# The even mixer's 31-tap convolution: chunks moved from GpSimd to TensorE, with diagonal tap tiles loaded from DRAM

## The chip, the cores and the metric

One program on one core of a Trainium2 chip. The metric is the device time of one execution in microseconds, the median of several runs. The engines are called PE (TensorE; PEld is its weight loads), DVE (VectorE), ACT (ScalarE), POOL (GpSimd) and SP (SyncE, which here only issues DMAs).

## The reference, cut to what matters

The network has a first block of two transformer layers with experts, and a second block of two layers, each of a mixer, a cross-attention to a memory and an MLP. The mixer of the second block's first layer is the "even" mixer; 256 tokens of 1024 channels, all in fp32:

```python
def causal_depthwise_conv(x, w, b):          # here: w is [31, 1024], one filter of 31 taps for each channel
    width = w.shape[0]
    y = lax.conv_general_dilated(x, w[:, None, :], window_strides=(1,), padding=[(width - 1, 0)],
                                 dimension_numbers=('NWC', 'WIO', 'NWC'), feature_group_count=x.shape[-1])
    return y + b

def even_mixer(x, w_in, conv_w, conv_b, ...):
    proj = x @ w_in                                        # 1024 -> 4624 columns
    conv_val, conv_gate, z, xbc, dt = jnp.split(proj, ...)
    u = conv_val * jax.nn.sigmoid(conv_gate)
    u = causal_depthwise_conv(u, conv_w, conv_b)           # the convolution of this change
    u = jax.nn.silu(layer_norm_2(u, conv_ln_g, conv_ln_b)) # normalised over the 1024 channels
    xbc = jax.nn.silu(causal_depthwise_conv(xbc, ...))     # four taps
    ...                                                    # the state-space branch: y, gated by silu(z), normalised
    return jnp.concatenate([u, y], axis=-1) @ w_out
```

Each output of the convolution is a sum of 31 products, out[n, ch] = sum over j of w[j, ch] u[n - 30 + j, ch], plus a bias. The channels stand on the partitions in eight chunks of 128.

## The kernel before, in words

`even` (from L1119) is one pass over the mixer. Its dense products split each fp32 weight tile into a high part `wh` (ACT, L252) and a low part `wl` (DVE, L255), and do three matmuls for each pair of tiles (L363 to L365, or L289 to L291). Weights come as tiles of 128x2048 fp32 (1 MB) through `raw` (L224): three buffers in rotation, loads issued by SP in program order, each waiting until the buffer's last tile has been read.

In program order: `wvg` (eight tiles) gives value and gate; ACT takes a tanh, and DVE writes the gated value into `U` (L1148), two chunks at a time, with 30 zeros ahead of each chunk. Then `xbc` with its four taps (L1164 to L1175), a chain of 128x32 instructions for dt (L1183 to L1198), `z` (`wz`, four tiles), the state-space branch (L1238 to L1286), the convolution (L1288 to L1324), its normalisation (L1326 to L1355: sums of the channels by matmuls with ones, L1329 and L1343) and the product with `weo` (eight tiles; the state-space half of its rows, `caty`, first, then the half of the convolution, `catu`, in the rows the tiles `xt`).

A scheduler puts each engine's instructions into a fixed order ahead of time, so the convolution's instructions stand between those of the dense products. The eight chunks go three ways (L1787, L1290, L1312):

- chunks 4 and 7 on PE (L1291 to L1310). `cpair0` and `cpair1` hold 64 channels each: on partitions 0 to 63 the chunk as it is, on 64 to 127 the same shifted by one position, so that one matmul of 128 rows does two taps. Its weights are two 64x64 diagonals of taps, one under the other, which ACT makes into `cdiag`, one instruction for each (L1304). 16 tap pairs by two halves are 32 matmuls for a chunk, and the trace holds two records for each matmul; the halves write different partitions of one accumulator.
- chunks 0 and 3 on POOL, a multiplication into `cvt` and an addition for each tap (L1314 to L1324).
- chunks 1, 2, 5 and 6 on DVE, one multiply-add for each tap (L1322).

Of the kernel before, what the change touches and what calls it, by code (L numbers as in the profile page):

```python
# [26 lines left out]
OP = mybir.AluOpType  # L27
# [69 lines left out]
def layout(inp):  # L97
    g = {k: np.asarray(v) for k, v in inp.items()}
    o = {}
# [66 lines left out]
    o["convw2"] = np.ascontiguousarray(w.reshape(16, 2, 8, 2, 64).transpose(1, 4, 2, 3, 0)).reshape(128, 256)  # L166
# [19 lines left out]
class Net:  # L186
# [46 lines left out]
    @contextmanager  # L233
    def more_raw(self, n, side="left"):
        """n more tiles for weights in flight, while the block lasts"""
        with self.tc.tile_pool(name="rawx", bufs=1, side=side) as pool:
            i = self.slot % len(self.slots)
            self.slots = self.slots[i:] + self.slots[:i] + [(pool, f"rx{j}") for j in range(n)]
            self.slot = 0
            yield  # L240
            i = self.slot % len(self.slots)
            self.slots = [x for x in self.slots[i:] + self.slots[:i] if x[0] is not pool]
            self.slot = 0
# [18 lines left out]
    def split_x(self, dst, src, scale=None):  # L262
        """dst (hi, lo) views <- src fp32 view (SBUF or PSUM)"""
        hi, lo = dst
        nc = self.nc
        if scale is None:
            nc.scalar.activation(hi, src, AF.Copy)
            nc.vector.tensor_tensor(lo, src, hi.bitcast(F32), op=OP.subtract)
        else:
            nc.scalar.activation(hi, src, AF.Copy, scale=scale)  # L270
            nc.vector.scalar_tensor_tensor(lo, src, scale, hi.bitcast(F32), op0=OP.mult, op1=OP.subtract)

    def affine_split(self, dst, src, G, B, n):
        """blocks: dst[:, k] <- src[:, k] * G[:, k] + B[:, k]; src PSUM [128, n, w]"""
        hi, lo = dst
        nc = self.nc
        x = self.wk.tile([128, n, src.shape[-1]], F32, tag="afs", name="afs", bufs=2)
        for k in range(n):
            if B is None:
                nc.scalar.activation(x[:, k], src[:, k], AF.Copy, scale=G[:, k:k + 1])  # L280
            else:
                nc.scalar.activation(x[:, k], src[:, k], AF.Identity, scale=G[:, k:k + 1], bias=B[:, k:k + 1])
        nc.vector.tensor_copy(hi, x)  # L283
        self.last_split = nc.vector.tensor_tensor(lo, x, hi.bitcast(F32), op=OP.subtract)  # L284
# [8 lines left out]
    def dense_nat(self, units, tiles, evac, ncol=512, kper=4):  # L293
        """units: list of (xh, xl, token offset); tiles: [[DRAM tile per K group] per column chunk]"""
# [23 lines left out]
    def project(self, us, src, qs, finish):  # L318
        """finish(u, c, acc) for the halves c of 1024 columns, unit by unit; src[c, q]: weights of the K groups q"""
# [24 lines left out]
    def dense_tr(self, x, tiles, evac, tag="acc"):  # L344
        """x: (hi, lo) [128, 8, 256]; tiles: DRAM [128, 8*256]; evac(tile, psum [128, 2, 256])"""
        for c, src in enumerate(tiles):
            acc = self.bank(tag).rearrange("p (b n) -> p b n", b=2)
            self.tile_tr(x, self.raw(src), acc)
            evac(c, acc)
# [17 lines left out]
    def transpose_into(self, src, n, sink, tags=("tp",)):  # L367
        """src [128, n*128] -> banks of four [128, 128] blocks; sink(block offset, count, psum)"""
# [14 lines left out]
    def half_stats(self, key, z, c):  # L383
        """statistics of the half c of the rows z"""
        if c == 0:
            self.bst[key] = self.wk.tile([128, 2, 6], F32, tag="bst", name="bst", bufs=5)
        self.nc.vector.bn_stats(self.bst[key][:, c], z[:, c * 512:(c + 1) * 512])

    @contextmanager
    def later(self, n):  # L390
        """work of the block as if it came n instructions later"""
# [4 lines left out]
    def row_stats(self, key, eps):  # L396
        """(mean and variance, 1 / standard deviation) of rows whose halves half_stats has seen"""
# [4 lines left out]
    def norm_rows(self, key, z, eps):  # L402
        """z <- (z - mean) * rsqrt(var + eps) along the free axis"""
# [6 lines left out]
    def last_rows(self, key, z, eps, g, b, out):  # L410
        """out <- the normalised rows z times g plus b"""
# [43 lines left out]
    def mods(self, l, i):  # L455
        """a third of the modulation vectors of both streams, as columns: eight steps, to call one after the other;
        the four column groups of the PE array take 512 columns each"""
# [23 lines left out]
    def mods_rows(self, l, i, n):  # L481
        """the same third for the first n streams, by the sums of products along the free axis"""
# [26 lines left out]
    def bc_cols(self, cols):  # L509
        """[128, 512] PSUM <- the 512 entries of the columns [128, 4], on every partition"""  # L510
# [5 lines left out]
    def bc(self, l, i, s, out):  # L516
        """out [128, 1024] <- the modulation vector i of stream s on every partition"""
# [65 lines left out]
    def rope_to(self, x, t, nh):  # L583
        """x [128, nh, 64]; the two addends of its rotation"""
# [14 lines left out]
    def mixers(self, mg, gp, pool, l, streams, with_ctx, hook):  # L599
        """streams: {name: (xh, xl)}; mg[stream, token tile] <- twice the merged branches"""  # L600
# [29 lines left out]
        def place_q(m, s, t, q):  # L630
            """q [128, 2, 128]: the heads of g=0 and of g=1"""
# [34 lines left out]
        def chunk(src, ncol, kper, evac_full, ctx_cols):  # L666
            """one column chunk for the streams that need all of it; the ctx stream may need only ctx_cols"""
# [62 lines left out]
        # branch A  # L730
# [38 lines left out]
        # branch B and the queries of C  # L769
# [92 lines left out]
    def router(self, pool, l, fold, streams):  # L862
        """router weights times the modulated gain, and what the mean and the shift of the rows add"""
# [18 lines left out]
    def route(self, pool, l, zT, wg, add, stats, streams):  # L882
        """one-hot columns of each expert's tokens and the affinities; zT[s, half]: the rows before their
        normalisation, transposed; stats[s, t]: their means and standard deviations"""
# [67 lines left out]
    def experts(self, l, z, fold, streams, g2, gain, oh, af, rsc):  # L952
        """z[s] [128, 2, 1024], normalised, becomes ALPHA * h + g2 * (the experts' outputs at their tokens)"""
# [151 lines left out]
    def small_tr(self, pool, x, w, name):  # L1105
        """[16, 256 tokens] in SBUF <- x @ w for 16 columns, transposed"""
# [12 lines left out]
    def even(self, pool, x, finish):  # L1119
# [4 lines left out]
        cw2 = self.load(pool, "convw2t", I["convw2"], [128, 8, 2, 16])  # L1124
        ident2 = mk("ident2", [128, 64])
        nc.vector.tensor_tensor(ident2, self.ident[:, 0:64], self.ident[:, 64:128], op=OP.add)
# [22 lines left out]
        # state-space branch  # L1149
# [139 lines left out]
        for k in range(8):  # L1289
            if k in self.conv_pe:  # L1290
                acc = self.bank("acc")[:, :256]  # L1291
                ps = []
                for h in range(2):
                    hs = slice(64 * h, 64 * h + 64)
                    p = mk(f"cpair{h}", [128, 286])
# [4 lines left out]
                for m in range(0, 16, 2):  # L1300
                    d = mk("cdiag", [128, 2, 2, 64], 2)
                    for h in range(2):
                        for i in range(2):
                            nc.scalar.activation(d[:, h, i], ident2, AF.Copy, scale=cw2[:, k, h, m + i:m + i + 1])  # L1304
                    for i in range(2):
                        for h in range(2):
                            q = m + i
                            nc.tensor.matmul(acc[64 * h:64 * h + 64], lhsT=d[:, h, i], rhs=ps[h][:, 2 * q:2 * q + 256],
                                             start=q == 0, stop=q == 15, skip_group_check=True)
                nc.scalar.activation(cv[:, k], acc, AF.Identity, scale=0.5, bias=cb[:, k:k + 1])  # L1310
                continue
            pool_k = k in self.conv_pool  # L1312
            eng = nc.gpsimd if pool_k else nc.vector
            eng.tensor_scalar(cv[:, k], U[:, k, 0:256], cw[:, k, 0:1], None, op0=OP.mult)  # L1314
            for j in range(1, 31):
                if pool_k:
                    tm = mk("cvt", [128, 256], 2)
                    nc.gpsimd.tensor_tensor(tm, U[:, k, j:j + 256], cw[:, k, j:j + 1].to_broadcast([128, 256]),
                                            op=OP.mult)
                    nc.gpsimd.tensor_tensor(cv[:, k], cv[:, k], tm, op=OP.add)  # L1320
                else:
                    nc.vector.scalar_tensor_tensor(cv[:, k], U[:, k, j:j + 256], cw[:, k, j:j + 1], cv[:, k],  # L1322
                                                   op0=OP.mult, op1=OP.add)
            eng.tensor_scalar(cv[:, k], cv[:, k], 0.5, cb[:, k:k + 1], op0=OP.mult, op1=OP.add)  # L1324

        # normalisation of the convolution over channels  # L1326
# [355 lines left out]
    def residual(self, z, g, b, side="left"):  # L1682
        """z <- z * g + b, in place"""
# [15 lines left out]
    def mem_kv(self, i):  # L1699
        """a quarter of the memory's keys or values, to DRAM until they are needed"""  # L1700
# [76 lines left out]
    def build(self):  # L1777
        tc = self.tc
        with ExitStack() as self.ctx:
# [7 lines left out]
            self.conv_pe, self.conv_pool = (4, 7), (0, 3)  # L1787
# [29 lines left out]
```

## Time and profile before

| | |
|---|---|
| three timed runs | 2828.42, 2828.75, 2834.20 us; median 2828.75 us |
| the profiled execution | span 2830.3 us |
| busy over the span | PE 2479.0 us, DVE 1554.4 us, ACT 856.9 us, POOL 296.6 us |
| mean clock granted to PE | 0.918 of full speed |

The profiled execution's own time is its span; what lies around the first and last instruction is not shown, and 2830.3 lies among the three timed runs. In the page's 40 slices of 70.8 us the even mixer is slices 27 to 30, which for POOL read 7, 9, 0, 0 tenths busy. The stretch from the first gated value to the last product with `weo` runs from about 1866 to 2117 us of the span.

### The profile page before, as it was taken

The numbers are of one execution on the slowest core, as the hardware profiler recorded it, in microseconds if no ns is written. First come the engines' busy times: TensorE is split into PE (matmuls) and PEld (weight loads), VectorE is DVE, ScalarE is ACT, GpSimd is POOL, SyncE is SP. The second block draws the span as 40 slices with busy tenths as digits, with TensorE's granted clock in tenths as the row PEclk, the third lists the DMA queues.
The fourth block names the chain that finished last, engine by engine and source line by source line (L and its number), as shares of the span: only waits on it lengthen the run. The fifth ranks groups of instructions, "written<-read, shape, count | busy, mean of one in ns | idle before, by whom it ended". The sixth has DMA issues, their size and how long they took to land.

```text
span 2830.3 us, 35061 instructions
## 1 busy us (share of the span) xinstructions
PE 2479.0 (88%) x14042; PEld 1694.2 (60%) x14042; DVE 1554.4 (55%) x2586; ACT 856.9 (30%) x1485; POOL 296.6 (10%) x261
## 2 busy tenths in 40 slices
PE   7999999899899879998866777786999999998898
PEld 4667678552222227776412333376768898867797
DVE  4779886442222258756311222289976755656655
ACT  2343233210000014533100010132664544543443
POOL 0001120000000011010000000079001100201100
PEclk8999999999989889999877878787999999998999
DMA  7135555489999964546899999842255652543551
GB/s 285 63 132 181 168 214 216 175 332 412 421 421 421 422 275 148 189 140 245 371 427 426 425 426 426 373 145 86 75 181 195 224 190 87 187 181 130 198 182 42
DMA packets 115811, 695.75 MB, mean 246 GB/s; under 512 B 26288, under 2 KB 27184, under 8 KB 34752
## 3 DMA queue, kind: packets, MB, share of 16 engines
q1 hardware_dynamic: 113728, 687.22, 62.5%
q0 software_dynamic: 1920, 6.29, 0.6%
q8 instruction: 111, 1.82, 0.3%
q14 instruction: 52, 0.43, 0.0%
HBM read 688.22 MB, written 5.24 MB: 245 GB/s over the span
## 4 chain that ended last, share of the span: by engine, by line
PE 61%; DMA 18%; DVE 14%; issue 3%; ACT 3%; POOL 1%; SPq 0%; DVEq 0%; POOLq 0%; ACTq 0%
PE acc L291 9%; PE acc L289 9%; PE acc L290 9%; DMA raw<-in_wgu 8%; PE acc L1005 8%; PE acc L1037 5%; DMA raw<-in_wdn 4%; DVE wl L255 3%; PE att L364 2%; DMA raw<-in_xwk 2%; PE att L365 2%; PE att L363 2%; PE att L552 2%; PE tp L373 2%; PE att L579 2%
## 5 line engine op out<-in xcount | busy, mean ns | idle before, releaser
L255 DVE TENSOR_TENSOR wl<-raw,wh 128x1024 fp32r<-128x1024 f32 x384 | 485.9, 1271 | 281.7 <-ACT wh L252 274.6
L252 ACT ACTIVATE wh<-raw 128x1024 fp32r<-128x1024 f32 x384 | 403.8, 1058 | 578.1 <-PE acc L291 257.5
L1005 PE MATMUL acc<-raw,xs 128*64 128x512 f32 (+1 forms) x2048 | 379.9, 648 | 58.6 <-DMA raw<-in_wgu 58.3
L1005 PEld LDWEIGHTS acc<-raw,xs 128*64 128x64 f32 (+1 forms) x2048 | 99.4, 126 | 307.3 <-issue 180.0
L1009 ACT ACTIVATE eth<-acc 64x512 f32<-64x512 f32 x48 | 28.3, 590 | 671.7 <-PE acc L1005 671.7
L1011 DVE SCALAR_TENSOR_TENSOR esg<-eth,acc 64x512 f32<-64x512 f32 x48 | 32.7, 680 | 351.2 <-ACT eth L1009 350.7
L289 PE MATMUL acc<-wh,xtlath 128*128 128x512 f32 (+1 forms) x448 | 177.2, 396 | 9.8 <-DVE xtlath L283 6.7
L380 POOL TENSOR_TENSOR rs<-rs,mhalf 128x1 f32<-128x1 f32 (+3 forms) x36 | 31.7, 885 | 1446.1 <-DVE rs L379 1444.5
L291 PE MATMUL acc<-wh,xtlatl 128*128 128x512 f32 (+1 forms) x448 | 177.3, 397 | 1.8 <-DVE xtlatl L284 1.8
L290 PE MATMUL acc<-wl,xtlath 128*128 128x512 f32 (+1 forms) x448 | 177.0, 395 | 1.4 <-DVE wl L255 1.4
L492 DVE SCALAR_TENSOR_TENSOR junk<-raw,crow 128x1024 bf16<-128x1024 f32 x128 | 162.9, 1273 | 5.0 <-DMA raw<-in_wmt 4.2
L364 PE MATMUL acc<-xth,wl 128*128 128x256 f32 x416 | 128.7, 309 | 36.6 <-DVE wl L255 36.5
L363 PE MATMUL att<-xth,wh 128*128 128x256 f32 x512 | 145.7, 285 | 6.7 <-DVE xth L283 6.7
L1037 PE MATMUL acc<-raw,eaT 128*64 128x512 f32 x512 | 141.7, 717 | 10.3 <-DVE eaT L202 5.5
L364 PE MATMUL att<-xth,wl 128*128 128x256 f32 x512 | 145.5, 284 | 0.3 <-DVE wl L255 0.3
L365 PE MATMUL att<-xtl,wh 128*128 128x256 f32 x512 | 145.4, 284 | 0.0
L363 PE MATMUL acc<-xth,wh 128*128 128x256 f32 x416 | 127.3, 306 | 8.0 <-DVE xth L283 8.0
L365 PE MATMUL acc<-xtl,wh 128*128 128x256 f32 x416 | 126.6, 305 | 5.3 <-DVE xtl L284 5.3
L364 PEld LDWEIGHTS acc<-xth,wl 128*128 128x128 f32 x416 | 89.0, 214 | 40.4 <-DVE wl L255 39.6
L1048 DVE TENSOR_TENSOR eylat<-acc,g2lat 32x512 f32<-32x512 f32 x32 | 21.9, 684 | 151.8 <-PE acc L1037 151.6
L363 PEld LDWEIGHTS att<-xth,wh 128*128 128x128 f32 x512 | 98.9, 193 | 7.6 <-issue 7.0
L289 PEld LDWEIGHTS acc<-wh,xtlath 128*128 128x128 f32 x448 | 85.7, 191 | 29.5 <-issue 10.2
(540 smaller groups left out, 5276.3 us busy)
## 6 DMA issues: line engine op xcount, KB each, us to landing
raw<-in_wgu SPq DMA_DIRECT2D x256, 1024.0 KB, 19.5
raw<-in_wdn SPq DMA_DIRECT2D x128, 1024.0 KB, 19.0
raw<-in_w SPq DMA_DIRECT2D x64, 1024.0 KB, 4.9
raw<-in_wmt SPq DMA_DIRECT2D x40, 1024.0 KB, 4.9
raw<-in_wgat SPq DMA_DIRECT2D x32, 1024.0 KB, 4.8
raw<-in_wmod SPq DMA_DIRECT2D x8, 1024.0 KB, 7.2
raw<-in_wqkv SPq DMA_DIRECT2D x8, 1024.0 KB, 10.7
wbr<-in_wbr SPq DMA_DIRECT2D x16, 512.0 KB, 5.3
```

The lines of the kernel that those rows point to most:

```text
L252: self.nc.scalar.activation(hi, s, AF.Copy)
L255: self.last_lo = self.nc.vector.tensor_tensor(lo, s, hi.bitcast(F32), op=OP.subtract)
L289: mm(out, lhsT=xh, rhs=wh, start=first, stop=False)
L290: mm(out, lhsT=xh, rhs=wl, start=False, stop=False)
L291: mm(out, lhsT=xl, rhs=wh, start=False, stop=last)
L363: mm(acc[:, b], lhsT=h[:, s], rhs=xh[:, k], start=k == 0, stop=False)
L364: mm(acc[:, b], lhsT=l[:, s], rhs=xh[:, k], start=False, stop=False)
L365: mm(acc[:, b], lhsT=h[:, s], rhs=xl[:, k], start=False, stop=k == 7)
L373: self.nc.tensor.transpose(t[:, j], src[:, (b + j) * 128:(b + j + 1) * 128], self.ident)
L492: nc.vector.scalar_tensor_tensor(junk, r[:, b * 1024:b * 1024 + 1024], 1.0, self.crow[:, s], op0=OP.mult, op1=OP.mult, accum_out=self.mcol ...
L1005: nc.tensor.matmul(o, lhsT=lt, rhs=w[:, a, c], start=k == 0, stop=k == 7)
L1037: nc.tensor.matmul(yb[64 * h:64 * h + 64], lhsT=aT[:, kf], rhs=w[:, f, h * 512:(h + 1) * 512], start=kf == 0, stop=kf == 7)
```

## The change

The host writes, for each chunk, all 32 diagonal pairs of 128x64 side by side: a tensor `convd` of eight tiles of 128x2048, of which five are read. PE takes chunks 1, 3, 4, 6 and 7, DVE takes 0, 2 and 5, POOL none. A chunk on PE loads its tile through `raw`; the `cdiag` instructions on ACT, `ident2` and the small tensor `convw2` go. `cpair` has two buffers for each half. (The diff also drops comments and docstrings, so that line numbers of the new kernel are up to 13 lower or 3 higher; those lines are left out here.)

```diff
@@ layout
-    o["convw2"] = np.ascontiguousarray(w.reshape(16, 2, 8, 2, 64).transpose(1, 4, 2, 3, 0)).reshape(128, 256)
+    taps = w.reshape(16, 2, 8, 2, 64).transpose(2, 4, 1, 0, 3)
+    diag = np.zeros((8, 64, 2, 16, 2, 64), np.float32)
+    diag[:, np.arange(64), :, :, :, np.arange(64)] = taps.transpose(1, 0, 2, 3, 4)
+    o["convd"] = np.ascontiguousarray(diag.transpose(0, 2, 1, 3, 4, 5)).reshape(8, 128, 2048)
@@ even
-        cw2 = self.load(pool, "convw2t", I["convw2"], [128, 8, 2, 16])
-        ident2 = mk("ident2", [128, 64])
-        nc.vector.tensor_tensor(ident2, self.ident[:, 0:64], self.ident[:, 64:128], op=OP.add)
...
-                    p = mk(f"cpair{h}", [128, 286])
+                    p = mk(f"cpair{h}", [128, 286], 2)
...
-                for m in range(0, 16, 2):
-                    d = mk("cdiag", [128, 2, 2, 64], 2)
+                d = self.raw(I["convd"][k]).rearrange("p (q h n) -> p q h n", q=16, h=2)
+                for q in range(16):
                     for h in range(2):
-                        for i in range(2):
-                            nc.scalar.activation(d[:, h, i], ident2, AF.Copy, scale=cw2[:, k, h, m + i:m + i + 1])
-                    for i in range(2):
-                        for h in range(2):
-                            q = m + i
-                            nc.tensor.matmul(acc[64 * h:64 * h + 64], lhsT=d[:, h, i], rhs=ps[h][:, 2 * q:2 * q + 256],
-                                             start=q == 0, stop=q == 15, skip_group_check=True)
+                        nc.tensor.matmul(acc[64 * h:64 * h + 64], lhsT=d[:, q, h], rhs=ps[h][:, 2 * q:2 * q + 256],
+                                         start=q == 0, stop=q == 15, skip_group_check=True)
...
-            pool_k = k in self.conv_pool
-            eng = nc.gpsimd if pool_k else nc.vector
...                                          (the POOL form of the taps goes, the DVE form stays)
@@ build
-            self.conv_pe, self.conv_pool = (4, 7), (0, 3)
+            self.conv_pe = (1, 3, 4, 6, 7)
```

On DVE the new order is the old one, from the first `U` to the state-space branch, but for two places where a tap and a `wl` change sides; the taps are those of other chunks. In both kernels this piece stands after a low part of `xbc` weights; `dtp`, `dt` and `dA` end the dt chain, `xcs` are the four taps, and `acs` waits for four matmuls of PE on `dA`:

```order
L1193 TENSOR_SCALAR dtp<-dtp 128x32
L1175 SCALAR_TENSOR_TENSOR xcs<-thx,xcs 128x512
L1194 TENSOR_TENSOR dtp<-dtp,dts 128x32
L1171 SCALAR_TENSOR_TENSOR xcs<-X,sconvwt,xcs 128x256
L1195 SCALAR_TENSOR_TENSOR dt<-dt,dtp 128x32
L1171 SCALAR_TENSOR_TENSOR xcs<-X,sconvwt,xcs 128x256
L1198 SCALAR_TENSOR_TENSOR dA<-dt,alogt 128x32
L1171 SCALAR_TENSOR_TENSOR xcs<-X,sconvwt,xcs 128x256
L1204 COPY acs<-att 128x32
L1205 TENSOR_SCALAR nacs<-att 128x32
L1207 TENSOR_TENSOR dend<-att,acs 128x16
```

Nothing has moved here. The end of the convolution does move. On DVE of the kernel before, the last taps stand between the low parts of the first `weo` tiles, ahead of the normalisation's `cv<-cv,cvt`:

```order
L1322 SCALAR_TENSOR_TENSOR cv<-U,convwt,cv 128x256 x9
L255 TENSOR_TENSOR wl<-raw,wh 128x1024
L1322 SCALAR_TENSOR_TENSOR cv<-U,convwt,cv 128x256 x3
L255 TENSOR_TENSOR wl<-raw,wh 128x1024
L1322 SCALAR_TENSOR_TENSOR cv<-U,convwt,cv 128x256
L1324 TENSOR_SCALAR cv<-cv,convbt 128x256
L255 TENSOR_TENSOR wl<-raw,wh 128x1024
L1340 TENSOR_TENSOR cv<-cv,cvt 128x512 x4
```

On DVE of the changed kernel the last tap is done before the second `z`, and the state-space branch and the low parts follow one another:

```order
L286 CAST xcs<-afs 128x4x128
L287 TENSOR_TENSOR catyl<-afs,xcs 128x4x128
L258 TENSOR_TENSOR wl<-raw,wh 128x1024 x4
L1327 TENSOR_TENSOR cv<-cv,cvt 128x512 x4
L1332 RECIPROCAL cvt<-cvt 128x256
L258 TENSOR_TENSOR wl<-raw,wh 128x1024
L1336 TENSOR_TENSOR cv<-cv,cvt 128x512 x4
```

So the taps have left this end of the DVE order. On PE of the kernel before, the convolution's matmuls come after the last one of `z`, in pieces among the sums (L1329), the transposes of the state-space output `y` and the first `weo` products:

```order
L1308 MATMUL acc<-cpair_13522,cdiag 64x256
L1329 MATMUL att<-cv,constt 128x256 x2
L1308 MATMUL acc<-cpair_13664,cdiag 64x256
L289 MATMUL acc<-wh,xcs 128x512
L373 MATMUL tp<-constt,y_13142 128x128 x8
L1308 MATMUL acc<-cpair_13668,cdiag 64x256
```

On PE of the changed kernel they begin at the same place, 160 of them, broken only by two groups of eight transposes (after 11 and after 43), and end like this:

```order
L1303 MATMUL acc<-cpair_13538,raw 64x256
L1303 MATMUL acc<-cpair_13542,raw 64x256
L1316 MATMUL att<-cv,constt 128x256 x8
L292 MATMUL acc<-wh,xcs 128x512
L293 MATMUL acc<-wl,xcs 128x512
L294 MATMUL acc<-wh,catyl 128x512
```

The eight sums and all 96 `caty` products now stand behind the convolution: eight products come between the sums and the eight sums of squares (L1330), and 88 after those. On SP of the changed kernel the five tiles stand between `wz` and `weo`, in the same three buffers:

```order
L233 DMA raw<-in_wxbc 128x2048 x6
L233 DMA raw<-in_wz 128x2048 x4
L233 DMA raw<-in_convd 128x2048 x5
L233 DMA raw<-in_weo 128x2048 x8
```

Before, `weo` came straight after `wz`; now its first tile waits until the third chunk has been read by PE.

## Rows read from the trace of the kernel before

**Rows 1.** The mixer's stretches, every engine (busy us, instruction count); clock, DMA share, rate last.
```profile
core 0: us, PE busy (x) PEld busy (x) DVE busy (x) ACT busy (x) POOL busy (x), PEclk, DMA share, GB/s
1866.00:1991.00 125.00, 89.86 (x624) 86.61 (x623) 122.27 (x158) 43.40 (x70) 113.72 (x124) 0.84 0.29 104
1991.00:2036.30 45.30, 45.19 (x265) 37.01 (x262) 41.86 (x79) 25.57 (x59) 0.00 (x0) 1.00 0.25 93
2036.30:2117.50 81.20, 74.40 (x369) 53.57 (x369) 61.12 (x98) 57.92 (x135) 4.44 (x7) 0.98 0.41 150
1926.00:1966.00 40.00, 19.33 (x104) 18.54 (x104) 39.25 (x60) 10.22 (x19) 39.13 (x47) 0.67 0.17 57
```

**Rows 2.** Waits of PE, 1866 to 1991 us: total us, times, longest.
```profile
PE acc L364 <- DVE wl L255: 30.9, 9, 9.6
PE att L1202 <- DVE dA L1198: 4.2, 1, 4.2
```

**Rows 3.** Groups of instructions on DVE, 1868 to 1985 us: busy us, mean ns.
```profile
L1322 DVE SCALAR_TENSOR_TENSOR cv<-U,convwt,cv 128x256 f32<-128x256 f32 x58 | 46.7, 836 | 0.3
L255 DVE TENSOR_TENSOR wl<-raw,wh 128x1024 fp32r<-128x1024 f32 x22 | 33.9, 1545 | 2.6 <-ACT wh L252 2.6
L1171 DVE SCALAR_TENSOR_TENSOR xcs<-X,sconvwt,xcs 128x256 f32<-128x256 f32 x24 | 19.5, 836 | 0.6 <-ACT xcs L1169 0.6
L1192 DVE TENSOR_TENSOR dtp<-dtp,dtq 128x32 f32<-128x32 f32 x7 | 4.6, 661 | 0.0
```

**Rows 4.** The same view of DVE, 1985 to 2070 us.
```profile
L1322 DVE SCALAR_TENSOR_TENSOR cv<-U,convwt,cv 128x256 f32<-128x256 f32 x62 | 27.9, 479 | 0.4
L255 DVE TENSOR_TENSOR wl<-raw,wh 128x1024 fp32r<-128x1024 f32 x14 | 17.0, 1218 | 1.2 <-ACT wh L252 1.1
...
L1171 DVE SCALAR_TENSOR_TENSOR xcb<-X,sconvwt,xcb 128x256 f32<-128x256 f32 x12 | 5.2, 472 | 0.0
...
L379 DVE TENSOR_SCALAR rs<-ss 128x2 f32<-128x2 f32 x2 | 0.3, 160 | 0.0
```

**Rows 5.** Timeline of DVE, 2030 to 2036 us: start, length, instruction.
```profile
2030.71 4.44 DVE L1322 SCALAR_TENSOR_TENSOR cv<-U,convwt,cv 128x256 f32<-128x256 f32 x11
```

**Rows 6.** Timeline of GpSimd, 1980 to 1990 us: start, length, instruction.
```profile
1983.81 1.32 POOL L1324 TENSOR_SCALAR cv<-cv,convbt 128x256 f32<-128x256 f32 x1
```

**Rows 7.** Timeline of PE: start, length, instruction.
```profile
1961.23 0.42 PE L364 MATMUL acc<-xth,wl 128*128 128x256 f32 x1
1961.45 0.41 PE L365 MATMUL acc<-xtl,wh 128*128 128x256 f32 x1
...
1966.46 0.28 PE L364 MATMUL acc<-xth,wl 128*128 128x256 f32 x1
1966.58 0.28 PE L365 MATMUL acc<-xtl,wh 128*128 128x256 f32 x1
...
2036.41 1.95 PE L1308 MATMUL acc<-cpair,cdiag 128*64 128x256 f32 x16
...
2056.58 6.02 PE L1308 MATMUL acc<-cpair,cdiag 128*64 128x256 f32 x46
...
2073.18 1.89 PE L1343 MATMUL att<-U,constt 128*128 128x256 f32 x8
```

**Rows 8.** Groups of instructions on PE, 2036.3 to 2117.5 us.
```profile
L1308 PE MATMUL acc<-cpair,cdiag 128*64 128x256 f32 x128 | 17.9, 392 | 0.6 <-ACT cdiag L1304 0.6
```

**Rows 9.** Waits of PE, 2036.3 to 2117.5 us.
```profile
PE acc L289 <- ACT wh L252: 3.5, 2, 2.4
```

**Rows 10.** Groups of instructions on ACT, 2036.3 to 2062.7 us.
```profile
L1304 ACT ACTIVATE cdiag<-ident,convw2t 128x64 f32<-128x64 f32 x56 | 14.4, 347 | 0.8 <-PE acc L1308 0.8
...
L1296 ACT ACTIVATE cpair<-U 64x286 f32<-64x286 f32 x2 | 0.9, 438 | 0.0
```

**Rows 11.** DMA issues, 1960 to 2100 us: KB each, median us to landing.
```profile
raw<-in_weo SPq DMA_DIRECT2D x8, 1024.0 KB, 4.8
```

More of the change, by code (lines that the diff above doesn't have):

```diff
@@ L1310, in even @@
                 nc.scalar.activation(cv[:, k], acc, AF.Identity, scale=0.5, bias=cb[:, k:k + 1])
                 continue
-            pool_k = k in self.conv_pool
-            eng = nc.gpsimd if pool_k else nc.vector
-            eng.tensor_scalar(cv[:, k], U[:, k, 0:256], cw[:, k, 0:1], None, op0=OP.mult)
+            nc.vector.tensor_scalar(cv[:, k], U[:, k, 0:256], cw[:, k, 0:1], None, op0=OP.mult)
             for j in range(1, 31):
[L1316 to L1323, printed above, removed]
@@ L1324, in even @@
-            eng.tensor_scalar(cv[:, k], cv[:, k], 0.5, cb[:, k:k + 1], op0=OP.mult, op1=OP.add)
+                nc.vector.scalar_tensor_tensor(cv[:, k], U[:, k, j:j + 256], cw[:, k, j:j + 1], cv[:, k],
+                                               op0=OP.mult, op1=OP.add)
+            nc.vector.tensor_scalar(cv[:, k], cv[:, k], 0.5, cb[:, k:k + 1], op0=OP.mult, op1=OP.add)
         b = self.bank("att")[:, :256]
```

## The prediction

> **What bounds the kernel now.** I read the engines over the mixer first, cut where its limit changes [rows 1]. Call 1866 to 1991 us stretch A (`wvg` and `xbc`), 1991 to 2036.3 B (`z` and the state-space branch), 2036.3 to 2117.5 C (convolution on PE, normalisation, `weo`); the rest of the span has nothing of the change. In A DVE is busy 122.3 of 125.0 us and POOL 113.7; PE is busy 89.9, at a mean granted clock of 0.84. In B PE is busy 45.2 of 45.3 at full clock, in C 74.4 of 81.2. So DVE bounds A, PE bounds B, and C is PE's but for 6.8 us.
>
> The waits say what A hangs on: PE waited 30.9 us in nine waits for `wl`, up to 9.6 us at a time, and once 4.2 us for `dA`, which ends the dt chain; both are DVE's [rows 2]. Then DVE's own groups. One tap (L1322) takes 836 ns in A and 479 after it, a `wl` 1545 against 1218, a tap of the short filter (L1171) 836 against 472, and the 128x32 instructions of the dt chain 661 where small ones later take 160 [rows 3, 4]. A run of 11 taps in B takes 4.44 us, 0.40 apart [rows 5]. The change of pace falls on the end of POOL's last tap instruction, 1983.8 + 1.3 = 1985.1 us [rows 6]: the two groupings are cut there. The same instructions on the same shapes take 1.3 to 4 times as long while POOL works on taps.
>
> **A: what leaves with POOL's work.** The order on DVE stays, so each instruction of A stands where it was. By the means, 58 x (836 - 479) = 20.7 us, 22 x (1545 - 1218) = 7.2, 24 x (836 - 472) = 8.7, and 14 dt instructions (seven of L1192 as shown, seven of its neighbour taken as alike) x (661 - 160) = 7.0: 43.6 us [rows 3, 4]. DVE's 122.3 become 79 at most; another few us lie in about 30 single instructions that I leave out. The 160 ns are of another small instruction; if dt instructions do not get faster, DVE keeps 7 us more.
>
> What is late next is PE. Its 624 records of A come 0.12 us apart at full clock (1966.46, 1966.58) and 0.22 at the lower level (1961.23, 1961.45) [rows 7]: 624 x 0.12 = 75 us of work. DVE at 75 to 79 and PE at 75 are level, each waiting for the other (PE for `wl`; DVE for accumulators, by way of ACT), so A ends above both. Where the order gives DVE more between two `wl` than the 24 x 0.12 = 2.9 us of matmuls that one `wl` feeds, PE waits. The dt chain is that place: after the last `U`, ten taps and eleven small instructions (10 x 0.40 + 11 x 0.16 = 5.8 us) before a `wl`; then six short taps and seven small ones (3.5); then the piece quoted with the change, nine DVE rows and a round trip by PE, about 4.5 with what follows it. With 1.1 for each `wl` that is 17 us, against some 9 to 10 of matmuls: 7 us of waits. I add 3 for a lowered clock after them, as after the long waits of now (0.67 over 1926 to 1966 [rows 1]). A = 75 + 7 + 3 = 85: a gain of 40. Bounds: 50, if PE never waits; 25, if PE stays as long busy as now (89.9) and waits 10.
>
> Twelve copies into `cpair` come into A on ACT, each at most 0.44 us by the group that survives [rows 10]: 4 to 5 us on an engine with 43.4 of 125 us busy. Behind them are `wh` copies; a late one delays PE by 2 us at worst, within the bounds.
>
> **B** keeps PE's order and PE's bound: 0. Here and in C, DVE loses its fourth chunk's 31 taps (12 us), which hid beside PE.
>
> **C: what PE takes on.** 128 records of the convolution now take 17.9 us of PE [rows 8]; five chunks are 5 x 64 = 320. The spacing is the term to choose. The first 16, whose diagonals were made long before, took 1.95 us: (1.95 - 0.39) / 15 = 0.104. The last 46 took 6.02, (6.02 - 0.39) / 45 = 0.125, but there ACT makes each diagonal in 0.35 us as they run, 56 of them in 14.4 us, 0.26 for two records [rows 7, 8, 10]. With all diagonals loaded I take 0.11, near the row without that limit: 320 x 0.11 = 35.2 us, 17.3 more than now; at 0.125 it is 40.0 and 22.1 more. A 128-column matmul of the same length comes (1.89 - 0.38) / 7 = 0.216 apart [rows 7]: the two 64-column halves run beside each other, and the halved spacing rests on that.
>
> The 6.8 us of waits in C, 3.5 of them for `wh` behind other ACT work [rows 9], largely go, as ACT loses the diagonals (and now copies of the `mem` inputs stand further behind `wh`). New ones come: PE reaches both groups of transposes of `y` early (1 us each); the last sum waits for ACT's copy of the last chunk (0.5), the squares for `cv - mean` (1.5). I take 4. C = 74.4 + 17.3 + 4 = 95.7, 14.5 more. Low end: no waits, and the lower clock's share back (0.02 x 81.2 = 1.6 us), +9; high end: 0.125 and waits of 9 us, +25.
>
> The loads: a tile lands 4.8 us after its issue [rows 11]. Three diagonal tiles find their buffers free once `wz` is split, in B; the fourth and fifth wait for the first and second chunk to be read, and a chunk takes 64 x 0.11 = 7 us, more than 4.8. `weo` queues behind: its first tile waits for the third chunk, its third for the fifth. While that third and the fourth land (9.6 us), PE has the sums and squares (32 x 0.216 = 7) and the two first tiles' 48 products of 512 columns, at twice the 0.12 of 256 columns (11): hidden. Without that cover, some 5 us.
>
> **Sum.** -40 + 0 + 14.5 = -25.5. It is made against the profiled execution, 2830.3 us; that lies 1.5 above the median of the runs, 2828.75, from which I take it off: 2803 us. Its own range, ends of A and C not together: 2790 to 2814.
>
> **Rivals.**
> *The clock stays low in A.* DVE and PE are level, so PE could stop often and briefly and be held at the lower level of 1.2 GHz for much of A, as now at 0.84. Against it: C has 6.8 us of waits in pieces and was granted 0.98 [rows 1]. A = 100, the time 2818. The Trainium skill ("TensorE: Matmul & The Clock Gate", section "A second HAM failure mode: psum-queue depth-cycling") says that frequent micro-idles between groups of matmuls make the clock swing between its two levels; by that rule this rival decides; the trace's C, with the waits just named, does not show it.
>
> *The added loads are on the path.* If the five tiles do not hide, each costs its landing less what PE still has to do: at most 5 x 4.8 = 24 us, and 12 if half stays covered: 2815. For it: one ring of three buffers serves all. Against: DMA's share of 0.25 in B and 0.41 in C [rows 1]. The Trainium skill ("SBUF — State Buffer", section "A bandwidth-pool intuition that's wrong (but worth ruling out)") calls HBM almost always the end-to-end bottleneck, which would speak against loading five more tiles in place of making the diagonals on ACT; the shares just named do not bear it out here.
>
> *The halves of the convolution do not run beside each other* once they are fed from a loaded tile for 160 matmuls on end: slower. At 0.216 the 320 records take 69 us in C, 34 more than I count: 2837. It decides from a spacing of 0.11 + 25.5 / 320 = 0.19. For it: only 16 records stand for 0.104. Against it: no run of records, ACT-paced or not, came slower than 0.14 on the mean (17.9 / 128), where 0.216 would have been 28 us.
>
> *POOL is not the cause, or its work's cost reappears elsewhere*: A keeps 125 and C pays 14.5: 2843. Against it: the common end of both at 1985.1.
>
> *PE fills up better*: A = 77 and C +11: 2792.
>
> **How the numbers follow.** The forecast 0.60; low clock 0.14; loads 0.07; halves 0.06; POOL not the cause 0.04; better 0.09. The time is the forecast's, 2803. For 8 in 10, the range takes most of the better case and reaches to the low clock's time: 2787 to 2818; outside lie the slower rivals, the worst of the low clock and the best of the better case. A measurement tells 0.2% (5.7 us) from no change. Faster than that: the forecast, the better case, the loads and nearly all of the low clock, 0.88. Within it 0.04, from the ends of the low clock and of the halves; slower 0.08.
>
> **What would show it.** In the new profile: taps on DVE near 480 ns throughout; the dt instructions near 0.2 us; PE's waits for `wl` in A around 8 to 12 us, not 30.9; the clock above 0.9 in A; from the first `U` to the last product of `z` about 130 us instead of 170; 320 convolution records in 35 us; no DMA of `convd` or `weo` among the waits of PE. Wrong are the forecast's terms if A is longer than 95, the spacing over 0.13, or PE stands idle for `weo`.

## The result and the profile after

The changed kernel took 2793.23 us (median of 4 runs, 2787.22 to 2797.49), the kernel before 2831.07 beside it on the same chip (4 runs): a ratio of 0.9865, 95% interval 0.9847 to 0.9883. That is 38 us less; forecast were 25.5 less and 2803 us, with a range of 2787 to 2818. The direction and the mechanism came as forecast and the time lies inside the range; the sizes of two terms were off, that of A's gain by 10 us.

Both profiles can be cut at the same four places: the first `U` (L1148), the last product of `xbc`, the last of `z`, the last of `weo` (each by its start).

| stretch | before, us | after, us | difference | forecast |
|---|---|---|---|---|
| ahead of the mixer | 1868.2 | 1864.2 | -3.9 | 0 |
| A, first `U` to last `xbc` | 122.3 | 72.6 | -49.7 | -40 |
| B, to the last `z` | 45.6 | 45.5 | -0.1 | 0 |
| C, to the last `weo` | 81.2 | 96.6 | +15.4 | +14.5 |
| behind the mixer | 713.0 | 709.6 | -3.4 | 0 |
| span | 2830.3 | 2788.6 | -41.7 | -25.5 |

The first row is scatter: the change does not touch that stretch, and over the profiles of this study it lasts between 1862.9 and 1872.2 us. The other four make 37.8.

The engines over A, B and C of the changed kernel (busy us and instruction count of PE, PEld, DVE, ACT, POOL; granted clock; DMA's share; GB/s), to be laid beside [rows 1]:

```profile
core 0: us, PE busy (x) PEld busy (x) DVE busy (x) ACT busy (x) POOL busy (x), PEclk, DMA share, GB/s
1864.00:1937.00 73.00, 72.48 (x605) 71.59 (x604) 71.47 (x157) 43.96 (x73) 0.00 (x0) 1.00 0.47 167
1937.00:1982.50 45.50, 45.50 (x268) 37.41 (x266) 41.33 (x74) 22.81 (x56) 0.00 (x0) 1.00 0.25 93
1982.50:2079.00 96.50, 90.09 (x562) 66.33 (x561) 51.74 (x72) 52.42 (x97) 4.22 (x7) 1.00 0.51 185
```

PE is now busy in 72.5 of A's 73 us, at a clock of 1.00 (2.4 GHz) where it had 0.84 between its two levels. DVE does nearly the same list of work in 71.5 us instead of 122. POOL stands at nothing. In C PE has 562 records instead of 369, and DVE, with 51.7 of 96.5 us, is half idle.

DVE's groups in A (busy us, mean ns), beside [rows 3], and all that PE waits for in A, beside [rows 2]:

```profile
L258 DVE TENSOR_TENSOR wl<-raw,wh 128x1024 fp32r<-128x1024 f32 x24 | 29.1, 1215 | 2.7 <-ACT wh L255 2.7
L1309 DVE SCALAR_TENSOR_TENSOR cv<-U,convwt,cv 128x256 f32<-128x256 f32 x59 | 26.2, 473 | 0.3
L1171 DVE SCALAR_TENSOR_TENSOR xcs<-X,sconvwt,xcs 128x256 f32<-128x256 f32 x24 | 10.9, 477 | 0.3 <-ACT xcs L1169 0.3
L1192 DVE TENSOR_TENSOR dtp<-dtp,dtq 128x32 f32<-128x32 f32 x7 | 1.3, 181 | 0.0
```
```profile
PE att L1202 <- DVE dA L1198: 0.5, 1, 0.5
```

A tap takes 473 ns instead of 836, a `wl` 1215 instead of 1545, a small instruction of the dt chain 181 instead of 661: close to what the kernel before showed once POOL had ended [rows 4]. Of 35.1 us of PE waits 0.5 are left.

In C, the convolution's records as a group, a run of them in the timeline, and PE's waits:

```profile
L1303 PE MATMUL acc<-cpair,raw 128*64 128x256 f32 x320 | 35.6, 379 | 0.0
```
```profile
1996.22 25.69 PE L1303 MATMUL acc<-cpair,raw 128*64 128x256 f32 x234
```
```profile
PE acc L292 <- ACT wh L255: 2.7, 2, 2.1
PE acc L293 <- DVE wl L258: 2.0, 3, 0.8
PE tp L376 <- DVE y L1284: 1.6, 2, 1.3
```

The records come (25.69 - 0.38) / 233 = 0.109 us apart; 320 of them keep PE busy 35.6 us. PE waits 6.3 us in C, and none of it is for a tile of `convd` or `weo`. The last 2.1 us of it, from 2068 on, are for a `wh` and a `wl` that come late because ACT, ahead of them, had waited 3.2 and 1.7 us for tiles of `mem`, which both kernels load. The clock of 1.00 in C is that of this profile: a second profile of the same kernel has 0.97 and a C of 98.4 us (experiment 11).

### The profile page after: what moved, and what is told of

Same layout as the page of the kernel before. It is cut to its first block, busy times and chain, and to the rows that moved or that the text cites. A ratio compares the mean times of both kernels' runs of the same rounds, so it can differ in the third digit from the quotient of the medians.

```text
span 2788.6 us, 35251 instructions
## 1 busy us (share of the span) xinstructions
PE 2475.7 (89%) x14234; PEld 1693.0 (61%) x14234; DVE 1495.0 (54%) x2553; ACT 850.0 (30%) x1442; POOL 183.3 (7%) x137
## 4 chain that ended last, share of the span: by engine, by line
PE 65%; DMA 17%; DVE 11%; issue 3%; ACT 2%; POOL 1%; SPq 0%; DVEq 0%; POOLq 0%; ACTq 0%
PE acc L294 9%; PE acc L293 9%; PE acc L292 9%; PE acc L1008 8%; DMA raw<-in_wgu 8%; PE acc L1040 5%; DMA raw<-in_wdn 3%; PE att L367 2%; PE att L368 2%; PE att L366 2%; DMA raw<-in_xwk 2%; PE att L555 2%; DVE wl L258 2%; PE acc L367 2%; PE acc L368 2%
## 5 line engine op out<-in xcount | busy, mean ns | idle before, releaser
L258 DVE TENSOR_TENSOR wl<-raw,wh 128x1024 fp32r<-128x1024 f32 x384 | 478.5, 1252 | 296.3 <-ACT wh L255 291.4
L367 PE MATMUL acc<-xth,wl 128*128 128x256 f32 x416 | 121.9, 293 | 4.0 <-DVE wl L258 4.0
L292 PE MATMUL acc<-wh,xtctxh 128*128 128x512 f32 (+1 forms) x272 | 102.7, 378 | 0.6 <-DVE th L729 0.6
```

What stands on the lines that cost most here:

```text
L258: self.last_lo = self.nc.vector.tensor_tensor(lo, s, hi.bitcast(F32), op=OP.subtract)
L292: mm(out, lhsT=xh, rhs=wh, start=first, stop=False)
L367: mm(acc[:, b], lhsT=l[:, s], rhs=xh[:, k], start=False, stop=False)
```

## The experiments

The theory after the result: POOL's taps slowed DVE's instructions with two inputs in SBUF, DVE held PE up, and with POOL idle PE bounds A at its full clock; C then pays what a chunk's records cost on PE. The rivals: the gain comes from less work on DVE, from ACT's freed time, or from loading the diagonals. All numbers of A and C below are cut as in the table.

**1. The two POOL chunks on DVE, nothing else (kernel before).**
```
-            self.conv_pe, self.conv_pool = (4, 7), (0, 3)
+            self.conv_pe, self.conv_pool = (4, 7), ()
```


> The kernel before with the two POOL chunks (0 and 3) put on DVE and nothing else: two chunks stay on PE with diagonals made by ACT, no chunk is loaded, DVE has six chunks instead of four. Theory (POOL's taps slow DVE, and that alone made stretch A long): taps near 480 ns in A, A 72 to 80 us instead of 122; B 45; C longer by about 16 us, because about 85 taps (35 us) and 10 us of work on y come after the last z before the channel sums can be made, against 30 us there now; total 2795 to 2812. Rival (A was long because DVE had too much work, or because ACT had): DVE has more work still, so A stays at 120 or more and the total is 2840 to 2860.

Measured 2802.21 us, 0.9892 of before (0.9877 to 0.9907). A 72.1, B 45.2, C 99.1. A and C in the windows view, and PE's waits in C:

```profile
1868.50:1940.70 72.20, 72.19 (x602) 71.31 (x601) 71.47 (x160) 41.66 (x66) 0.00 (x0) 1.00 0.48 168
1985.90:2085.20 99.30, 75.82 (x370) 54.80 (x368) 80.93 (x152) 55.68 (x134) 3.81 (x6) 0.90 0.31 117
```
```profile
PE att L1329 <- DVE cv L1324: 17.8, 1, 17.8
PE acc L289 <- ACT wh L252: 2.1, 1, 2.1
```

A comes out as in the changed kernel, to half a microsecond, though DVE has more convolution to do over the mixer, not less (in A itself it is busy 71.5 us in both), and nothing is loaded. So the whole of A's gain is POOL's absence. What the further chunks on PE are for shows in C: here PE stands 17.8 us before the channel sums for the end of DVE's last chunk, and C is granted 0.90 on the mean.

**2. POOL's taps put back into the changed kernel, their sums unused.**
```
+            if k in (0, 3):
+                cx = mk("cvx", [128, 256])
+                nc.gpsimd.tensor_scalar(cx, U[:, k, 0:256], cw[:, k, 0:1], None, op0=OP.mult)
+                for j in range(1, 31):
+                    tm = mk("cvt", [128, 256], 2)
+                    nc.gpsimd.tensor_tensor(tm, U[:, k, j:j + 256], cw[..., j:j + 1]..., op=OP.mult)
+                    nc.gpsimd.tensor_tensor(cx, cx, tm, op=OP.add)
```


> The changed kernel, with the tap work of chunks 0 and 3 that POOL did before given back to POOL in the same place, its sums unused (chunks 0 and 3 come from where the changed kernel takes them). Theory (contention): taps on DVE back to about 830 ns while POOL works, A back to 110 to 122 us, clock in A below 0.9, total 2793 + 40 to 50 = 2833 to 2843. Rival (the gain came from the one chunk less on DVE or from the order of work): A stays under 85 and the total within 8 us of 2793.

Measured 2842.78 us. A 122.4, C 98.7. DVE's tap and PE's waits in A:

```profile
L1317 DVE SCALAR_TENSOR_TENSOR cv<-U,convwt,cv 128x256 f32<-128x256 f32 x60 | 48.2, 832 | 0.3
```
```profile
PE acc L367 <- DVE wl L258: 32.8, 10, 9.6
PE att L1202 <- DVE dA L1198: 4.1, 1, 4.1
```

Work that nobody uses makes the program some 50 us slower and restores A to the tenth of a microsecond, down to the 9.6 us of PE's longest wait [rows 2]. With experiment 1 this is shown from both sides.

**3. POOL busy, but writing only.**
```
+            if k in (0, 3):
+                cx = mk("cvx", [128, 512])
+                nc.gpsimd.tensor_scalar(cx[:, 0:256], U[:, k, 0:256], cw[:, k, 0:1], None, op0=OP.mult)
+                for j in range(90):
+                    nc.gpsimd.memset(cx, 0.0)
```


> The changed kernel with POOL busy in stretch A on writes alone: two tensor_scalar that read U, then 180 memsets of 128x512 on one tile that nobody uses. If DVE is slowed only by POOL instructions that read SBUF, as the Trainium skill has it (SBUF - State Buffer, section Who interferes with whom): taps stay near 480 ns, A at 73 us, total 2788 to 2798. If any POOL access to SBUF slows DVE: taps at 700 ns or more while the memsets run, A over 95 us, total over 2815.

Measured 2793.8 us, A 74.7. POOL's work, and four groups of DVE beside it:

```profile
L1294 POOL MEMSET cvx<- 128x512 f32 x180 | 94.9, 527 | 10.4
```
```profile
L1314 DVE SCALAR_TENSOR_TENSOR cv<-U,convwt,cv 128x256 f32<-128x256 f32 x90 | 40.9, 476 | 0.9
L258 DVE TENSOR_TENSOR wl<-raw,wh 128x1024 fp32r<-128x1024 f32 x30 | 36.5, 1222 | 3.6 <-ACT wh L255 3.6
L1193 DVE TENSOR_SCALAR dtp<-dtp 128x32 f32<-128x32 f32 x7 | 2.4, 345 | 0.0
L1312 DVE TENSOR_SCALAR cv<-U,convwt 128x256 f32<-128x256 f32 x3 | 1.4, 474 | 0.0
```

POOL works for 95 us and the taps stay at 476 ns, `wl` at 1222: neither POOL's being busy nor its writing slows them. What POOL's taps have beside that is reading. The Trainium skill ("SBUF — State Buffer", section "Who interferes with whom") says that a DVE instruction with two SBUF inputs contends with a GpSimd instruction that reads SBUF, not with one that only writes; the two groups agree. It also says that instructions such as `tensor_scalar` may take both port pairs and then contend with any access of GpSimd; the last two groups agree: L1193 takes 345 ns here against 172 in the changed kernel, the one-input tap 474 against 346. Counted from the first `U`, `dA` is done 0.6 us later, and A is 2 us longer. Most of that is the clock, which falls after a wait of 0.5 us for a `wl` and one for `dA`:

```profile
1918.00:1920.50 2.50, 2.50 (x14) 2.50 (x13) 2.50 (x3) 1.07 (x2) 2.29 (x4) 0.50 0.31 46
```

The trace lists the wait for `dA` with 1.7 us, but it lists 1.7 in experiments 5 and 7 too, where A is 72.6: in all three a dozen records just ahead of it are missing, and by an estimate some 0.4 us of it are a wait (1.7 - 12 x 0.11).

Two groups tell the same of the reads. Over A they keep their time while POOL's taps run (three of the four L1148 stand beside taps); first the kernel before, then the changed one:

```profile
L1148 DVE SCALAR_TENSOR_TENSOR U<-thx,acc 128x512 f32<-128x512 f32 x4 | 2.7, 676 | 0.0
L1148 DVE SCALAR_TENSOR_TENSOR U<-thx,acc 128x512 f32<-128x512 f32 x4 | 2.7, 678 | 0.0
```

L1148 takes one of its two inputs from `acc`, PE's accumulator, and not from SBUF. The other is the `RECIPROCAL` of the dt chain, which has one input: 341 ns before, 336 after.

**4. Five chunks on PE, diagonals made by ACT.**
```
-                d = self.raw(I["convd"][k]).rearrange("p (q h n) -> p q h n", q=16, h=2)
+                for m in range(0, 16, 2):
+                    d = mk("cdiag", [128, 2, 2, 64], 2)
+                    for h in range(2):
+                        for i in range(2):
+                            nc.scalar.activation(d[:, h, i], ident2, AF.Copy, scale=cw2[:, k, h, m + i:m + i + 1])
```


> The changed kernel with the diagonal tiles of its five PE chunks made by ACT as before (64 copies of 128x64 a chunk at 0.26 us for two records) instead of loaded. Theory (loading is a small part, worth only the spacing of the records in C): A and B unchanged at 73 and 46; in C the spacing goes from 0.108 to 0.125 to 0.135, so 5 to 9 us more, partly offset by diagonals made ahead; total 2796 to 2803. Rival (loading the diagonals is what freed A, by ACT's time): A grows by 10 us or more and the total is over 2806.

Measured 2809.44 us, 0.9922 (0.9906 to 0.9939). A 72.6, B 45.3 as expected, but C 111.1: 14.5 us more, where 5 to 9 were expected. (It is 32 copies a chunk, not the 64 that the expectation says.) ACT's diagonals while the convolution runs, and all engines over the same 1983.5 to 2041 us:

```profile
L1304 ACT ACTIVATE cdiag<-ident,convw2t 128x64 f32<-128x64 f32 x152 | 38.4, 340 | 1.0 <-PE acc L1308 0.9
1983.50:2041.00 57.50, 51.72 (x358) 28.16 (x358) 15.84 (x32) 53.61 (x199) 1.42 (x2) 1.00 0.05 19
```

The convolution's stretch takes 56 us here, 39 with loaded tiles. ACT is the bound, busy 53.6 of 57.5 us: 38.4 of diagonals, and its other work between them. I had taken the pace of the diagonals by themselves, 0.125. So loading is no part of the gain in A, but it is what makes five chunks on PE pay: worth 14.5 of C.

**5. Four chunks on PE.** **6. Three chunks on PE.** The rest on DVE.
```
-            self.conv_pe = (1, 3, 4, 6, 7)
+            self.conv_pe = (1, 4, 6, 7)      # 5
+            self.conv_pe = (3, 6, 7)         # 6
```


> The changed kernel with four chunks on PE (1, 4, 6, 7) and four on DVE (0, 2, 3, 5). Theory (PE bounds A, B and C, a chunk on PE costs 64 records at 0.108 = 6.9 us in C, and a chunk on DVE is free as long as it ends before PE needs it): C 6 us shorter, 90 to 91; A and B unchanged at 73 and 46; total 2785 to 2789. Rival (DVE's last taps, some 35 after the last z, 14 us, with 10 us of work on y, end after the 256 records, 28 us, and PE waits for cv): C 95 to 98, total 2792 to 2796.

> The changed kernel with three chunks on PE (3, 6, 7) and five on DVE. By the run with six chunks on DVE, where PE waited 17.8 us in C for the last cv, DVE is late here too: its taps after the last z (55, 22 us), the work on y (10) and the wl among them (11) take 43 us, against 192 x 0.108 = 21 us of records and 4 of transposes; PE waits 8 to 18 us, so C is 2 us shorter to 5 longer than with five chunks, total 2790 to 2799. Rival (PE fills the time with the products of weo that need y alone): 14 us shorter, total 2779 to 2783.

Measured: four chunks 2787.34 us, 0.984 (0.9826 to 0.9853); three chunks 2789.64 us, 0.985 (0.9836 to 0.9863). A 72.6 in both, C 91.8 and 89.7. PE's waits in C, with four and with three:

```profile
PE acc L292 <- ACT wh L255: 3.6, 2, 2.1
PE acc L293 <- DVE wl L258: 1.3, 2, 0.8
PE tp L376 <- DVE y L1284: 1.0, 1, 1.0
```
```profile
PE acc L292 <- ACT xth L270: 6.7, 1, 6.7
PE acc L292 <- ACT wh L255: 1.4, 1, 1.4
PE tp L376 <- DVE y L1284: 1.1, 1, 1.1
PE att L1316 <- DVE cv L1311: 0.9, 1, 0.9
```

The fourth DVE chunk is free: C loses 4.8 us of the 6.9 that its records cost, and 7.4 between the profiles of experiments 11 and 12. (The granted clock of C differs: 1.00 with five chunks above, 0.96 with four, 0.94 with three.) The fifth comes late: PE waits 6.7 us for `xth`, which is made from the normalised convolution. Less than the 8 to 18 expected, because PE takes the products of `weo` that need `y` alone meanwhile; but the next 6.9 us of records bring only 2.1, no more than two profiles of one kernel differ by.

**7. Both halves of a convolution product in the same 64 columns.** The convolution's bias is left out here.
```
-                        nc.tensor.matmul(acc[64 * h:64 * h + 64], lhsT=d[:, q, h], ...
+                        nc.tensor.matmul(acc[0:64, 256 * h:256 * h + 256], lhsT=d[:, q, h], ...
```


> The changed kernel with both 64-column halves of each convolution product sent to the same 64 columns of the PE array (rows 0 to 63 of the accumulator, 256 columns for each half), two copies of 64 rows by ACT in place of one of 128; the bias of the convolution is left out. Theory (the spacing of 0.108 is that of two halves that run beside each other in different columns): spacing 0.21 to 0.22, 320 records in 68 us instead of 35 and C 130 us, total 2793 + 34 = 2825 to 2830. Rival (a 64-column record costs half of a 128-column one by itself): spacing stays at 0.11 and the total within 5 us of 2793.

Measured 2827.21 us; A 72.6, C 132.8. A run of the records, to be read beside that of the changed kernel above:

```profile
1995.66 39.66 PE L1303 MATMUL acc<-cpair,raw 128*64 128x256 f32 x183
```

(39.66 - 0.38) / 182 = 0.216 us apart, twice the 0.109, the length of a record unchanged: the price of a chunk rests on two halves that run beside each other in different columns of the array. The rival with the halves is right about its price, 34 us, and wrong that it decides here.

**8. The kernel before with loaded diagonals for its two PE chunks.** `cpair` has two buffers, as in the changed kernel.
```
-                            nc.scalar.activation(d[:, h, i], ident2, AF.Copy, scale=cw2[...])
+                d = self.raw(I["convd"][k]).rearrange("p (q h n) -> p q h n", q=16, h=2)
```


> The kernel before with the diagonals of its two PE chunks loaded from DRAM instead of made by ACT; POOL and DVE keep their chunks. Theory (contention in A is untouched, loading saves only in C): A 122, B 46; in C the 128 records at 0.108 take 14 us instead of 17.9, and the run with ACT diagonals in five chunks lost 14.5 us in C, 2.9 a chunk, so C 3 to 7 us shorter: total 2825 to 2829. Rival (loading carries a good part of the 38 us): total under 2815.

Measured 2832.14 us, 0.9997 (0.9988 to 1.0007): no difference. A 121.5, C 75.4, so C is 5.8 us shorter, as expected, and that is lost again at once: behind C 719.1 us are left instead of 713.0. PE's waits just behind C, here and in the kernel before:

```profile
PE tp L376 <- DVE zlat L410: 3.8, 1, 3.8
PE acc L367 <- DVE wl L258: 2.2, 1, 2.2
```
```profile
PE tp L373 <- DVE zlat L407: 1.7, 1, 1.7
PE acc L364 <- DVE wl L255: 0.3, 1, 0.3
```

On DVE the normalisation of `zlat` stands behind a `memxl`, which waits for ACT's copy of a `mem` tile, and ACT waits for the tile's load (timelines of DVE and of ACT, idle time before and its releaser in brackets):

```profile
2115.63 0.69 DVE L271 TENSOR_TENSOR memxl<-mem,memxh 128x512 fp32r<-128x512 f32 x1 [5.54 <-ACT memxh L270]
```
```profile
2114.97 0.63 ACT L270 ACTIVATE memxh<-mem 128x512 fp32r<-128x512 f32 x1 [9.36 <-DMA mem<-in_memT]
```

What counts is how late these copies come against the end of C. In the changed kernel the last `memxh` begins at 2069.59, 9.3 us ahead of the last `weo` product, and 709.6 us are left behind C. Over the profiles with four buffers of `wl`, the stretch behind C is 707.9 to 711.7 us where that lead is 9 us or more (at least four chunks on PE); with a lead of 4.9 it is 713.0 (before), with 3.8 it is 713.4 (experiment 6), with 1.6 it is 717.8 (experiment 1), and here, 3.4 us late, 719.1. The length of C by itself does not order them: C of experiment 1 is 99.1. So some 3 us of what PE takes on in C come back behind it. This is read from the order of the profiles; no run moved the copies alone.

**9. Three buffers for `wh` and `wl` instead of four. 10. Two.** Read for A alone: the buffers serve the whole second block.
```
-        with tc.tile_pool(name="spps", bufs=4) as self.spp, ...
+        with tc.tile_pool(name="spps", bufs=3) as self.spp, ...     # 10: bufs=2
```


> The changed kernel with three buffers each for wh and wl in the second block instead of four; read for stretch A alone. DVE's order in A is nearly the one of the changed kernel. There the wl that ends at 1901.47, before the dt chain, is used by PE only from 1909.74, and the next, which ends 7.1 us later, from 1912.62: PE lived on three wl made ahead (8.6 us). Theory (that stock is why the 7 us of waits that the prediction put at the dt chain did not come): with one buffer less the stock is at most two wl behind the one in use, 5.8 us against the chain's 7.1 us without a wl, so PE waits 1 to 5 us for wl or dA there and A is 74 to 80 us. Rival (the waits did not come because DVE's chain is faster than reckoned, or in another order, whatever the stock): waits under 1 us, A 72.6.

> The same with two buffers each for wh and wl; read for stretch A alone, where DVE's order differs more. Theory (the stock carries PE over the dt chain): one wl ahead at most, 2.9 us; PE waits 5 to 15 us in A, the clock falls below 1.00 there and A is 80 to 95. Rival (stock does not matter): A under 75.

Measured: three buffers 2839.19 us, A 72.9 with 0.2 us of waits; two buffers 2942.96 us, A 97.5. PE's waits in A with two:

```profile
PE acc L367 <- DVE wl L258: 15.3, 16, 2.1
```

With three my expectation failed: there is no wait at the dt chain, as the rival had it, and three buffers are enough for A. (In C the same run waits 4.8 us at once for a `wh`, and C is 107.8.) With two A is longer than the 80 to 95 us expected, and the waits are spread over A in 16 pieces and not heaped up at the dt chain. So PE needs some `wl` made ahead; that a stock of them carries it over the dt chain is not shown by these two runs, and rests on the timeline given further down.

**11. and 12. The changed kernel and the version with four chunks on PE once more, side by side.**

> The changed kernel once more, beside the next on the same chip, to compare the two: 2788 to 2796.

> Four chunks on PE, four on DVE, once more: C is 4.8 us shorter than with five in the profiles so far, so 4 to 6 us less than the run before, 2784 to 2790. If the gain is given back behind the mixer, as it was with the two loaded chunks, there is no difference.

Measured 2796.28 us (2792.77 to 2799.98) and 2788.85 us (2782.73 to 2789.82): 7 us apart, and no run of either lies in the range of the other. C is 98.4 and 91.0. Four chunks on PE beat both kernels: 0.9844 of before (0.9828 to 0.986).

The changed kernel's C is 1.8 us longer here than in its first profile, though PE waits no longer (5.7 us, the longest wait 2.1). The clock differs: it falls after the wait of 2.1 us and again after two of 1.0 and 0.8. C as a whole and the two stretches:

```profile
1988.30:2086.70 98.40, 92.58 (x562) 68.31 (x560) 51.85 (x72) 52.21 (x97) 4.22 (x7) 0.97 0.50 186
2054.50:2057.50 3.00, 2.62 (x7) 2.08 (x7) 3.00 (x4) 2.52 (x3) 0.00 (x0) 0.50 0.00 0
2078.00:2081.00 3.00, 3.00 (x8) 2.18 (x8) 2.44 (x3) 0.00 (x0) 0.00 (x0) 0.50 0.55 158
```

## Why the prediction was right, and where its sizes were off

**DVE bounds A because POOL slows it: right.** The new means (473, 1215, 477, 181) are those that were read behind POOL's end [rows 4], to 2%, but for the dt instructions, where 160 of another instruction stood for 181. Experiments 1 and 2 show the cause, experiment 3 takes POOL's writes out of it, which leaves its reads. The rival that POOL is not the cause is refuted.

**A = 75 + 7 + 3: the term that was mis-sized.** PE's 75 us are right; measured are 72.6 to the start of the last record. The 7 us of waits at the dt chain and the 3 of a lowered clock after them measured 0.5 and 0. A's gain of 49.7 is the prediction's own bound for a PE that never waits, 50. The delays on DVE were there. Its timeline round the chain in the changed kernel:

```profile
1898.53 1.21 DVE L258 TENSOR_TENSOR wl<-raw,wh 128x1024 fp32r<-128x1024 f32 x1
...
1900.26 1.21 DVE L258 TENSOR_TENSOR wl<-raw,wh 128x1024 fp32r<-128x1024 f32 x1
...
1907.33 1.22 DVE L258 TENSOR_TENSOR wl<-raw,wh 128x1024 fp32r<-128x1024 f32 x1
...
1911.51 1.22 DVE L258 TENSOR_TENSOR wl<-raw,wh 128x1024 fp32r<-128x1024 f32 x1
...
1916.07 0.18 DVE L1198 SCALAR_TENSOR_TENSOR dA<-dt,alogt 128x32 f32<-128x32 f32 x1
```

Between the ends of two `wl`, 1901.47 and 1908.55, lie 7.1 us, and 4.2 to the next: 11.3 us in which one `wl` comes to PE, 24 x 0.12 = 2.9 us of matmuls. PE did not stop, so at 1901.5 it had at least 11.3 - 2.9 = 8.4 us of matmuls in hand. I had summed DVE's pieces against the matmuls of the same pieces, as if PE came to the chain with nothing made ahead. Ahead of the chain DVE is the faster of the two and fills the buffers. Experiment 10 shows that PE needs `wl` made ahead; how small the stock at the chain may be stays open, as three buffers made no wait there.

**The rival of the low clock** fell with the waits: the granted clock of A is 1.00, in both profiles of the changed kernel. The rule of the Trainium skill ("TensorE: Matmul & The Clock Gate", section "A second HAM failure mode: psum-queue depth-cycling") that micro-idles between groups make the clock swing had no idles to act on in A. In C it does show, otherwise than the prediction read it: there the 0.98 of the kernel before, taken as speaking against the rival, is a clock at full but for one fall after waits of 2.4 and 0.8 us,

```profile
2109.00:2112.00 3.00, 2.69 (x6) 2.15 (x7) 2.23 (x4) 0.63 (x1) 0.00 (x0) 0.52 0.79 216
```

and the changed kernel's C stayed at 1.00 through eight waits of at most 2.1 us in one profile and fell to 0.50 twice in the other (experiment 11). So short waits do cost clock here, not every time, and what kept A clear of it is that PE did not stop. The prediction's reason against this rival was weaker than it looked.

**B: right**, 45.5.

**C = 74.4 + 17.3 + 4: right in sum.** The spacing of 0.11 measured 0.109, and PE's convolution 35.6 instead of 35.2. Waits measured 6.3, not 4; the largest is the one for `wh` that the prediction took to go (2.7 of 3.5 stay [rows 9]), and the clock gave back what was put at the low end: by luck, as the second profile has 0.97 and C 98.4. The loads hid, as worked out: with five more tiles on the ring PE waits for none of them, nor for `weo`. The rival of the loads fell; DMA's share of C is 0.51, and experiment 4 shows that making the tiles instead costs 14.5 us more. The sentence of the Trainium skill ("SBUF — State Buffer", section "A bandwidth-pool intuition that's wrong (but worth ruling out)") that HBM is almost always the bottleneck does not hold in this stretch.

**Behind C:** taken as 0, measured -3.4; it goes with the `mem` copies, which now come earlier against the end of C (experiment 8). With A's 10 us this is why 38 came and not 25.5; the better case, "A = 77 and C +11, 2792", had the total right by two terms that are each off.

## What to carry to other kernels

Where the same instruction on the same shape has two durations in one profile, look at what the neighbouring engine does in between, and count its reads: here 114 us of GpSimd work that reads SBUF cost the stretch that DVE bounds 50 us, though PE never waited for GpSimd in it. When a slow stretch of one engine meets a faster one, count what has been made ahead before you book a wait. And once one engine bounds a stretch from end to end, move work back to the idle one until it is just late: here that is a fourth chunk on DVE, 6 us better.

## What was not expected of the hardware

GpSimd's writes leave two-input DVE instructions alone (476 ns a tap beside 95 us of memsets), yet double a one-input `tensor_scalar` of 128x32 (345 against 172 ns). And GpSimd's tap work costs a small two-input instruction more than a large one: 128x32 goes from 181 to 661 ns, 480 more, a tap of 128x256 from 473 to 836, 363 more, a `wl` of 128x1024 from 1215 to 1545, 330 more; an instruction with one of its two inputs in `acc` loses nothing (L1148, experiment 3). One-input instructions differ: beside the tap work the `RECIPROCAL` keeps its time, a `tensor_scalar` of 128x32 (L1193) goes from 172 to 648 ns. One POOL tap instruction lasts 910 to 950 ns on the mean in experiment 2; a DVE instruction seems to wait for one of them to end, whatever its own size. That is read from the durations and was not tested by itself.
